# Kept PSUM banks, moved modulation vectors, phase tables by columns on VectorE: a two-layer DiT block on one Trainium2 core

## The chip, the core and the metric

The kernel runs on one core of a Trainium2 chip. A core has TensorE (PE, matmuls into eight PSUM banks of 128 partitions x 512 fp32), VectorE (DVE), ScalarE (ACT), GpSimd (POOL) and SyncE (SP), and 16 DMA engines fed from the queues of SP, ACT and POOL. Each engine works through its own instructions in order and waits on semaphores for the others. The metric is the device time of one execution in microseconds; lower is better.

## What is computed

A network of two layers on 1024 latent tokens and 256 context tokens, width 1024, all in fp32:

```python
for l in range(2):
    mod_l = (silu(c) @ ada_w[l] + ada_b[l]).reshape(b, 6, 1, 1024)      # shift, scale, gate, twice
    h_l = modulate(rmsnorm(x, norm1_g[l]), mod_l[:, 0], mod_l[:, 1])
    o = mla_retention_mixer(...) if l == 0 else s5_mixer(...)
    x = x + mod_l[:, 2] * o
    h_l = modulate(rmsnorm(x, norm2_g[l]), mod_l[:, 3], mod_l[:, 4])
    x = x + mod_l[:, 5] * (square(relu(h_l @ mlp_w1[l])) @ mlp_w2[l])
```

Layer 0 does the same for the context tokens with `mod_c`. The mixer of layer 1 is an S5 state space scan, in both directions, followed by a gated product:

```python
xs = associative_scan(a_bar * x + b_bar u)          # complex, 64 groups of 64 states, per direction
y = einsum('btgp,ghp->btgh', xs, c_mat).real
za, zb = split(gelu(y + d_skip * u) @ w_glu, 2)
out = za * sigmoid(zb)
```

## The kernel before, in words

Every large product is made of three matmuls on split operands (`mm3`): a number is the sum of a high part, rounded by ScalarE, and a low part, the difference, made by VectorE or GpSimd (`hi` and `lo`, line 84). Splitting a weight tile `mraw` gives `uh`, `ul` (first MLP weight, and the weight of the gated product) or `dh`, `dl` (second MLP weight).

The stages follow each other: layer 0's mixer (to about 1090 us), layer 0's MLP (to 2118), the S5 scan (2146 to 2335), the gated product (to 2522), layer 1's MLP (to the end).

`mlp` runs over 16 groups G of two hidden blocks. `first(G)` multiplies the normalised input by two blocks of the first weight, then ReLU and square on ScalarE (`r`, line 1042, and `ah`) and the low part `al` on GpSimd. `second(G-1)` multiplies by the second weight, two blocks deep, into one bank for each of eight output blocks, and VectorE adds each bank, times the modulation, to `x` (line 1064). Layer 0 calls it twice: first for 512 latent and 256 context tokens, then for the other 512 latent tokens. Each bank of `bank()` is one of six in turn (tag `b`); two more (`z`) serve the scan.

Beside layer 0's MLP runs a generator, `side`: the modulation of layer 1 (`ada_rest`: loads `aw` of the transposed weight, multiplied and summed along the row by VectorE, line 215), then the S5 tables: `s5_base` (many small VectorE instructions), `s5_outputs` (GpSimd products `oc`, joined by VectorE at 1383 and 1384, stored to `cst`) with `s5_lags` (small matmuls, stored to `tst`), `s5_inputs` (loads `wb` and `ww`, GpSimd products `wo`, joined by VectorE at 1341 and 1347, stored to `bst`) and `s5_tables` (phases `ta`, `tq`, their sines on ScalarE, stored to `csd`), then two norms. `beat` calls it at a rate of steps per matmul (`RA` in the first call, `RB` in the second), and `later(n, f)` puts a piece off by n steps. From the program so written, the framework makes the order of each engine's instructions at build time; it is that order, not the text, that the engines follow.

`s5_main` takes 32 pairs of groups, two directions each. `states`: TensorE makes `vb` from `ut` and `B`, VectorE turns it by the phase table `CS` (1486), adds two halves (1487), runs two scans (1491), GpSimd multiplies by the table again (`sy`, 1493) and adds two halves (`sa`, 1498; every fourth on VectorE). `outs`: TensorE multiplies `sa` by `C` and `ut` by `T` into banks `z` and `b`, two pairs behind. The `sy` tiles go round three. `glu` transposes the result, splits it (`yh`, `yl`), and makes 16 products of eight `mm3` for each half of the tokens; ScalarE and VectorE gate them and GpSimd adds them to `x`.

Of the kernel before, what the change touches and what calls it, by code (L numbers as in the profile page):

```python
# [9 lines left out]
F32 = mybir.dt.float32  # L10
# [41 lines left out]
class Net:  # L52


    def __init__(self, tc, I, out, tap=None):
        self.tc, self.nc, self.I, self.out = tc, tc.nc, I, out
        self.tap = tap or (lambda *a, **k: None)
        self.top = ExitStack()
        self.gelu = AF.Gelu_apprx_tanh

# [4 lines left out]
    def bank(self, tag="b"):  # L65
        return self.psum.tile([P, 512], F32, tag=tag, name=tag, bufs={"b": 6, "z": 2}[tag])
# [125 lines left out]
    def ada_row(self, tile):  # L192

        r = []
        for s in range(2):
            for k in range(2):
                t = tile(f"silr{s}{k}")
                self.nc.gpsimd.dma_start(
                    t, self.I["crow"][s, 512 * k:512 * k + 512].unsqueeze(0).to_broadcast([P, 512]))
# [4 lines left out]
    def ada_rest(self, tile, rows, todo):  # L204
        nc, I = self.nc, self.I
        for l, j in todo:
            ns = 2 if (l == 0 or j < 2) else 1
            for kt in range(KT):
                for k in range(2):
                    w = tile()  # L210
                    nc.sync.dma_start(w, I["adat"][l, j, kt, :, 512 * k:512 * k + 512])
                    for s in range(ns):
                        m = self.M[:, l, j, kt, s:s + 1]
                        o = w if s == ns - 1 else tile()
                        nc.vector.tensor_tensor_reduce(o, w, rows[2 * s + k], 1.0,
                                                       m if k else self.bias[:, l, j, kt:kt + 1],
                                                       ALU.mult, ALU.add, m)
                    if ns == 2 or k:
# [5 lines left out]
    def rows(self, parts, n):  # L224
# [12 lines left out]
        r = self.bank()  # L237
# [775 lines left out]
    def mlp(self, l, p, chunks, hget, x, beat=lambda w: None, done=None, last=iter(()), after=None, pre=iter(())):  # L1013

        nc, I = self.nc, self.I

# [34 lines left out]

        def second(G, A, w2):
            for t0, n, s in chunks:
                for oc in range(KT):
                    b = self.bank()
                    for fi in range(2):
                        self.mm3(b[:, :n], w2[fi](oc), A[fi, t0], fi == 0, fi == 1)
                    xs = x(oc, t0, n)
                    as_x = (lambda a: a[:, :n]) if len(xs.shape) == 2 else (lambda a: a.rearrange("p (t c) -> p t c", c=P))
                    o = xs  # L1060
                    if G == 15 and done:
                        res = p.tile([P, 512], F32, tag="r", name="res", bufs=2)
                        o = as_x(res)
                    nc.vector.scalar_tensor_tensor(o, as_x(b), self.M[:, l, 5, oc, s:s + 1], xs,  # L1064
                                                   op0=ALU.mult, op1=ALU.add)
                    if G == 15 and done:
# [761 lines left out]
```

## Time and profile before

| | us |
|---|---|
| median of 3 runs (3220.97 to 3245.53) | 3233.07 |
| profiled execution | 3247.53 |
| its span | 3245.7 |
| TensorE busy | 2982.2 (92%) |
| VectorE busy | 2172.1 (67%) |
| ScalarE busy | 1216.8 (37%) |
| GpSimd busy | 1059.6 (33%) |
| mean granted TensorE clock | 0.95 |

A page of the profile first gives the busy time of each engine, then the span in 40 slices of 81 us with a digit for the busy share in tenths. The granted clock is the part of full speed that the throttle let TensorE have. A row of a group reads: line, engine, operation, output <- inputs, shape, count, then busy time and mean nanoseconds of one, then the idle time of the engine just ahead of them and what ended it. A row of a wait reads: who <- whom, microseconds in total, times, longest. A row of a timeline reads: start, duration, engine, line, what, and in brackets the idle time ahead.

### The profile page before, as it was taken

To read this page: it belongs to the slowest core of one execution; us is meant where nothing else is said; L and a number is where in the kernel's file an instruction comes from. 1 tells how busy PE (TensorE), PEld (TensorE's weight loads), DVE (VectorE), ACT (ScalarE), POOL (GpSimd) and SP (SyncE) were. 2 spreads that over 40 slices of the span, in tenths; PEclk is the share of its full clock that TensorE was granted. 3 is DMA by queue.
4 is the path that set the end of the run, shared out by engine and by line. 5 is a ranking of instruction groups with operands and counts; after the bars stand their busy time and mean duration, and the time that the engine had idled before them with its cause. 6 is when DMAs were issued, how large, how long until landed. Compare 5 with 4: busy or idle time off the path is not lost. (4 is left out here: it accounts for less than half of the span.)

```text
span 3245.7 us, 43332 instructions
## 1 busy us (share of the span) xinstructions
PE 2982.2 (92%) x15659; PEld 2447.9 (75%) x15659; DVE 2172.1 (67%) x3899; ACT 1216.8 (37%) x2487; POOL 1059.6 (33%) x1012
## 2 busy tenths in 40 slices
PE   5899998899999999899987799956799999999998
PEld 3777777778878788788876577845588788888887
DVE  6777776687764599756666886479834555555555
ACT  6542322566662322222233455331244422222221
POOL 3642222355450111336526740146522111111111
PEclk8999997899999999999988899977799999999999
DMA  7132222210011356224437556278522111111111
GB/s 248 71 115 83 79 75 62 74 35 25 13 58 60 124 180 212 82 87 122 136 102 210 174 166 144 82 170 201 158 91 91 52 52 52 46 52 46 46 46 65
DMA packets 251927, 323.63 MB, mean 100 GB/s; under 512 B 71504, under 2 KB 166512, under 8 KB 251712
## 3 DMA queue, kind: packets, MB, share of 16 engines
q1 hardware_dynamic: 236432, 293.49, 30.5%
q10 hardware_dynamic: 14272, 24.38, 2.4%
q0 software_dynamic: 1008, 2.99, 0.3%
q8 instruction: 123, 2.02, 0.3%
q14 instruction: 92, 0.75, 0.1%
HBM read 267.43 MB, written 53.35 MB: 99 GB/s over the span
## 5 line engine op out<-in xcount | busy, mean ns | idle before, releaser
L1064 DVE SCALAR_TENSOR_TENSOR x<-b,mods,x 128x512 f32<-128x512 f32 (+1 forms) x624 | 531.4, 876 | 123.0 <-PE b L72 116.9
L84 POOL TENSOR_TENSOR al<-r,ah 128x512 fp32r<-128x512 f32 (+1 forms) x160 | 215.8, 1361 | 1110.4 <-ACT r L1046 1049.0
L70 PE MATMUL b<-ah,dh 128*128 128x512 f32 (+1 forms) x1280 | 481.1, 376 | 24.2 <-DVE x L1064 14.9
L71 PE MATMUL b<-al,dh 128*128 128x512 f32 (+1 forms) x1280 | 476.5, 372 | 0.7 <-POOL al L84 0.7
L72 PE MATMUL b<-ah,dl 128*128 128x512 f32 (+1 forms) x1280 | 474.6, 371 | 0.0
L84 DVE TENSOR_TENSOR ul<-mraw,uh 128x512 fp32r<-128x512 f32 x256 | 204.8, 805 | 388.8 <-ACT uh L76 388.2
L76 ACT ACTIVATE uh<-mraw 128x512 fp32r<-128x512 f32 x256 | 160.8, 629 | 447.2 <-PE b L71 272.7
L72 PE MATMUL b<-h2h,ul 128*128 128x512 f32 (+1 forms) x768 | 283.9, 370 | 35.9 <-DVE ul L84 35.9
L70 PEld LDWEIGHTS b<-ah,dh 128*128 128x128 f32 x1280 | 245.3, 192 | 74.7 <-DVE x L1064 22.1
L70 PE MATMUL b<-h2h,uh 128*128 128x512 f32 (+1 forms) x768 | 284.2, 370 | 14.1 <-ACT uh L76 9.2
L71 PE MATMUL b<-h2l,uh 128*128 128x512 f32 (+1 forms) x768 | 281.0, 366 | 0.0
L71 PEld LDWEIGHTS b<-al,dh 128*128 128x128 f32 x1280 | 245.2, 192 | 41.9 <-POOL al L84 1.1
L72 PEld LDWEIGHTS b<-ah,dl 128*128 128x128 f32 x1280 | 244.3, 191 | 41.5
L84 POOL TENSOR_TENSOR pl<-pe,ph 128x512 fp32r<-128x512 f32 (+1 forms) x128 | 158.8, 1250 | 155.5 <-ACT ph L76 83.8
L76 ACT ACTIVATE dh<-mraw 128x512 fp32r<-128x512 f32 x192 | 117.3, 627 | 238.1 <-PE b L71 222.9
L70 PE MATMUL b<-h3h,uh 128*128 128x512 f32 x512 | 202.2, 396 | 0.0
L71 PE MATMUL b<-h3l,uh 128*128 128x512 f32 x512 | 200.4, 392 | 2.0 <-DVE h3l L312 1.7
L72 PE MATMUL b<-h3h,ul 128*128 128x512 f32 x512 | 201.4, 394 | 0.0
L72 PEld LDWEIGHTS b<-h2h,ul 128*128 128x128 f32 x768 | 149.2, 194 | 65.6 <-DVE ul L84 41.3
L1042 ACT ACTIVATE r<-b 128x512 f32<-128x512 f32 (+1 forms) x160 | 88.0, 550 | 258.8 <-PE b L72 184.8
L70 PEld LDWEIGHTS b<-h2h,uh 128*128 128x128 f32 x768 | 149.0, 194 | 42.7 <-ACT uh L76 11.4
L70 PE MATMUL z<-wh,hh 128*128 128x512 f32 (+1 forms) x400 | 163.1, 408 | 12.6 <-ACT scr L496 6.3
(419 smaller groups left out, 6922.0 us busy)
## 6 DMA issues: line engine op xcount, KB each, us to landing
mraw<-in_w SPq DMA_DIRECT2D x192, 512.0 KB
aw<-in_adat SPq DMA_DIRECT2D x160, 256.0 KB
mraw<-in_glu SPq DMA_DIRECT2D x32, 512.0 KB
CS<-csd SPq DMA_DIRECT2D x32, 320.0 KB
w<-in_adaw SPq DMA_DIRECT2D x32, 256.0 KB
wraw<-in_winr SPq DMA_DIRECT2D x32, 256.0 KB
cst<-oc SPq DMA_DIRECT2D x64, 128.0 KB
wb<-in_s5bt ACTq DMA_DIRECT2D x32, 256.0 KB
```

The source lines that it names most:

```text
L70: mm(o, s[0], m[0], start=start, stop=False)
L71: mm(o, s[0], m[1], start=False, stop=False)
L72: mm(o, s[1], m[0], start=False, stop=stop)
L76: self.nc.scalar.activation(o, x, AF.Copy)
L84: e.tensor_tensor(o, x, h.bitcast(F32), ALU.subtract)
L1042: nc.scalar.activation(r[:, :n], b[:, :n], AF.Relu)
L1064: nc.vector.scalar_tensor_tensor(o, as_x(b), self.M[:, l, 5, oc, s:s + 1], xs, op0=ALU.mult, op1=ALU.add)
```

## The change

- *Banks.* The eight banks become `b` x 4, `c` x 2, `z`, `y`. Outside the layer 0 MLP a ring of six (`bbbbcc`) is handed out as before. Inside, three banks (`c`, `c`, `z`) hold running sums over all 16 groups: six of the eight context blocks in the first call, two to a bank, and three of eight latent blocks in the second. These are added to `x` once, at the end. Everything else rotates over the four `b`.
- *Modulation.* Vectors 3, 4 and 5 of layer 1 leave the side work and are made during the gated product, in loads and sums of 256 columns instead of 512.
- *Tables.* VectorE computes the phases group by group, with the frequency as a scalar; GpSimd has no part in it any more.
- *Queues and delays.* Loads of `s5_inputs` are issued by SP one part ahead (from ACT, in step, before); the stores of `bst`, `cst`, `tst` and `csd` are issued by ACT (SP before). Joins come two steps later (one before), stores five or four (three or two).
- *Scan.* The two halves of `sy` are no longer added; TensorE takes both, with twice as many matmuls. Every third product `sy` is VectorE's. `sy` goes round six tiles, `st` two.

```diff
+        self.ring, self.turn = "bbbbcc", 0
     def bank(self, tag="b"):
-        return self.psum.tile([P, 512], F32, tag=tag, name=tag, bufs={"b": 6, "z": 2}[tag])
+        if tag == "b":
+            self.turn = (self.turn + 1) % len(self.ring)
+            tag = self.ring[self.turn]
+        return self.psum.tile([P, 512], F32, tag=tag, name=tag, bufs={"b": 4, "c": 2, "z": 1, "y": 1}[tag])
...
+        keep, room = {}, 0
+        if kept:
+            self.ring = "bbbb"
+            for t0, n, s in chunks:
+                for oc in range(KT):
+                    if (t0, oc) in kept:
+                        if not room:
+                            bank, room = self.bank("ccz"[len(keep) * n // 512]), 512
+                        keep[t0, oc] = bank[:, 512 - room:512 - room + n], room == 512, room == n
+                        room -= n
...
         def second(G, A, w2):
+            open_ = []
             for t0, n, s in chunks:
                 for oc in range(KT):
-                    b = self.bank()
+                    b, opens, closes = keep.get((t0, oc)) or (self.bank()[:, :n], True, True)
+                    held, end = (t0, oc) in keep, G == 15
                     for fi in range(2):
-                        self.mm3(b[:, :n], w2[fi](oc), A[fi, t0], fi == 0, fi == 1)
...
+                        self.mm3(b, w2[fi](oc), A[fi, t0], fi == 0 and opens and not (held and G),
+                                 fi == 1 and closes and (end or not held))
+                    if end or not held:
+                        open_.append((oc, t0, n, s, b, end))
+                        if closes:
+                            while open_:
+                                add(*open_.pop(0))
...
-            gp.tensor_tensor(t3(a), ib, fb(0), ALU.mult)
-            gp.tensor_tensor(t3(l), ib, fb(1), ALU.mult)
+            for k in range(n):
+                v.tensor_scalar(q[:, cols[k]], self.io, fr[0][k], MAGIC, ALU.mult, ALU.add)
+            v.tensor_scalar(t2(q), t2(q), MAGIC, None, ALU.subtract)
+            for k in range(n):
+                v.scalar_tensor_tensor(a[:, cols[k]], self.io, fr[0][k], q[:, cols[k]], op0=ALU.mult, op1=ALU.subtract)
             yield
-            v.tensor_scalar(t2(q), t2(a), MAGIC, MAGIC, ALU.add, ALU.subtract)
-            v.tensor_tensor(t2(a), t2(a), t2(q), ALU.subtract)
-            v.tensor_tensor(t2(a), t2(a), t2(l), ALU.add)
+            for k in range(n):
+                v.scalar_tensor_tensor(a[:, cols[k]], self.io, fr[1][k], a[:, cols[k]], op0=ALU.mult, op1=ALU.add)
...
-                    nc.sync.dma_start(self.csd[:, g0:g0 + n, 1], t3(q))
+                    nc.scalar.dma_start(self.csd[:, g0:g0 + n, 1], t3(q))
...
+        nx = fetch(*parts[0])
+        for _ in range(4):
+            yield
+        for k, (d, g0) in enumerate(parts):
+            b, w = nx
+            if k + 1 < len(parts):
+                nx = fetch(*parts[k + 1])
+            qs = slice(g0 // 2, g0 // 2 + 4)
+            for r in range(2):
+                x, t = (self.atile(name="wo") for _ in range(2))
+                nc.gpsimd.tensor_tensor(x, w[0], b[r], ALU.mult)
                 yield
...
+                nc.gpsimd.tensor_tensor(t, w[1], b[1 - r], ALU.mult)
+                self.later(2, lambda r=r, x=x, t=t: nc.vector.tensor_tensor(
+                    x, x, t, ALU.add if r else ALU.subtract))
+                self.later(5, lambda qs=qs, d=d, r=r, x=x: nc.scalar.dma_start(self.bst[:, qs, d, r], gpv(x)))
...
-                self.later(1, join)
+                self.later(2, join)
...
+                e = gp if (2 * q + d) % 3 else v
+                e.tensor_tensor(y if d == 0 else y[:, :, :, ::-1],
+                                z[:, :, 31:159].unsqueeze(2).to_broadcast([P, 2, 2, P]), cs[:, :, ::-1, 31:159],
+                                ALU.mult)
+                A[q, d] = y
...
-                for w in range(2):
+                for r, w in ((0, 0), (1, 0), (0, 1), (1, 1)):
...
+                        if kt % 4 == 3:
+                            next(side, None)
...
-            yield from self.ada_rest(lambda: self.atile(name="aw"), rows, [(1, j) for j in range(6)])
+            yield from self.ada_rest(lambda: self.atile(name="aw"), rows, [(1, j) for j in range(3)])
...
+                     kept=[(1024, oc) for oc in range(6)])
...
+                     kept=[(512, oc) for oc in range(3)])
...
+                yield from self.ada_rest(a256, self.ada_row(a256, 1, 256), [(1, 4), (1, 3), (1, 5)], 256)
```

`fetch` issues the four loads of a part, two `wb` and two `ww`, on SP. `add` is the addition to `x` as it stood in `second` before.

What this makes of the engines' orders, at three places. VectorE in the second call of layer 0's MLP, at the phase tables; before:

```order
L1303 TENSOR_SCALAR tq<-ta 128x480
L1304 TENSOR_TENSOR ta<-ta,tq 128x480
L1303 TENSOR_SCALAR tq<-ta 128x480
L84 TENSOR_TENSOR ul<-mraw,uh 128x512
L1305 TENSOR_TENSOR ta<-ta,tl 128x480
L1304 TENSOR_TENSOR ta<-ta,tq 128x480
L1306 TENSOR_SCALAR ta<-ta 128x480
L1305 TENSOR_TENSOR ta<-ta,tl 128x480
L84 TENSOR_TENSOR ul<-mraw,uh 128x512
L1306 TENSOR_SCALAR ta<-ta 128x480
```

And now (`fr` holds the frequencies, `io` the column numbers):

```order
L1328 TENSOR_SCALAR tq<-tq 128x480
L1330 SCALAR_TENSOR_TENSOR ta<-io,fr_12297,tq 128x160 x3
L1333 SCALAR_TENSOR_TENSOR ta<-io,fr_12298,ta 128x160 x3
L1327 TENSOR_SCALAR tq<-io,fr_12297 128x160
L1334 TENSOR_SCALAR ta<-ta 128x480
L1327 TENSOR_SCALAR tq<-io,fr_12297 128x160 x2
L88 TENSOR_TENSOR ul<-mraw,uh 128x512
L1328 TENSOR_SCALAR tq<-tq 128x480
L1330 SCALAR_TENSOR_TENSOR ta<-io,fr_12297,tq 128x160 x3
L1333 SCALAR_TENSOR_TENSOR ta<-io,fr_12298,ta 128x160 x2
L88 TENSOR_TENSOR ul<-mraw,uh 128x512
```

The four instructions of a table group have become eleven, some rows standing for two or three; the splits `ul` and the adds lie between them as before.

VectorE at the end of the scan and the start of the gated product; before:

```order
L1487 TENSOR_TENSOR st<-st 128x320 x2
L1491 SCALAR_TENSOR_TENSOR sz<-R_13200,st 128x160 x4
L1486 TENSOR_TENSOR st<-b,CS 128x640 x2
L1487 TENSOR_TENSOR st<-st 128x320 x2
L1491 SCALAR_TENSOR_TENSOR sz<-R_13200,st 128x160 x4
L1498 TENSOR_TENSOR sa<-sy 128x2x128
L84 TENSOR_TENSOR yl<-b,yh 128x512
L84 TENSOR_TENSOR ul<-mraw,uh 128x512
L84 TENSOR_TENSOR yl<-b,yh 128x512
L84 TENSOR_TENSOR ul<-mraw,uh 128x512
L84 TENSOR_TENSOR yl<-b,yh 128x512 x6
```

And now (an `aw` row is one sum of 256 columns, a `mods` row reads its result out):

```order
L1518 TENSOR_TENSOR st<-st 128x320 x2
L1522 SCALAR_TENSOR_TENSOR sz<-R_12294,st 128x160 x4
L220 ISA aw,mods<-aw,silr_22764,adab 128x256
L220 ISA mods 128x1
L1525 TENSOR_TENSOR sy<-sz,CS 128x4x128
L220 ISA aw,mods<-aw,silr_22767,mods 128x256
L220 ISA mods 128x1
L220 ISA aw,mods<-aw,silr_22764,adab 128x256
L220 ISA mods 128x1
L220 ISA aw,mods<-aw,silr_22770,mods 128x256
```

29 such sums now stand between the last scan and the first `yl`, with the last `sy`, now VectorE's, behind the first of them.

SP at the same place, the loads; before:

```order
L1454 DMA B<-bst 128x512
L1456 DMA CS<-csd 128x2x320
L1457 DMA C<-cst 128x512
L1460 DMA T<-tst 128x1x128 x2
L1003 DMA mraw<-in_glu 128x1024 x32
```

And now:

```order
L1487 DMA CS<-csd 128x2x320
L1488 DMA C<-cst 128x512
L1491 DMA T<-tst 128x1x128 x2
L216 DMA aw<-in_adat 128x256 x29
L1008 DMA mraw<-in_glu 128x1024 x3
L216 DMA aw<-in_adat 128x256 x3
L1008 DMA mraw<-in_glu 128x1024
L216 DMA aw<-in_adat 128x256 x6
```

29 loads for the sums stand ahead of the first weights of the gated product, and more of them between the weights that follow. Elsewhere, of the 32 joins of `s5_inputs` in VectorE's order, 13 now stand in groups 11 and 12 of the first call and 19 at the border between the two calls.

More of the change, by code (lines that the diff above doesn't have):

```diff
@@ L188, in ada_first, with ada_row @@
         self.gains(0, 0)
-    def ada_row(self, tile):
+    def ada_row(self, tile, ns=2, n=512):
         r = []
-        for s in range(2):
-            for k in range(2):
+        for s in range(ns):
+            for k in range(1024 // n):
                 t = tile(f"silr{s}{k}")
                 self.nc.gpsimd.dma_start(
-                    t, self.I["crow"][s, 512 * k:512 * k + 512].unsqueeze(0).to_broadcast([P, 512]))
+                    t, self.I["crow"][s, n * k:n * k + n].unsqueeze(0).to_broadcast([P, n]))
                 self.nc.scalar.activation(t, t, AF.Silu)
@@ L208, in ada_rest @@
             for kt in range(KT):
-                for k in range(2):
+                for k in range(nk):
                     w = tile()
-                    nc.sync.dma_start(w, I["adat"][l, j, kt, :, 512 * k:512 * k + 512])
+                    nc.sync.dma_start(w, I["adat"][l, j, kt, :, n * k:n * k + n])
                     for s in range(ns):
@@ L236, in rows @@
         yield
-        r = self.bank()
+        r = self.bank("b" if len(self.ring) > 4 else "y")
         for j in range(n // P):
@@ new lines, in s5_inputs, with fetch @@
+        parts = [(d, g0) for d in range(2) for g0 in range(0, 64, 8)]
+        def fetch(d, g0):
+            b, w = ([self.atile(name=nm) for _ in range(2)] for nm in ("wb", "ww"))
+            for r in range(2):
+                nc.sync.dma_start(b[r], bass.AP(
+                    tensor=I["s5bt"].tensor, offset=I["s5bt"].offset + (d * 2 + r) * 4096 + g0 * 64,
+                    ap=[[0, 8], [16384, 16], [1, 512]]))
+                nc.sync.dma_start(w[r], bass.AP(
+                    tensor=self.pbd.tensor, offset=self.pbd.offset + (d * 16 + r) * 4096 + g0 * 64,
+                    ap=[[8192, 8], [0, 16], [1, 512]]))
+            return b, w
@@ L1414, in s5_lags @@
         v.tensor_tensor(E[:, 112:P], E[:, 112:P], b[:, P:144], ALU.add)
-        self.later(2, lambda: nc.sync.dma_start(self.tst[4 * it:4 * it + 4].rearrange("g h k -> (g h) k"), E))
+        self.later(4, lambda: nc.scalar.dma_start(self.tst[4 * it:4 * it + 4].rearrange("g h k -> (g h) k"), E))
     def s5_gen(self, gp):
@@ L1514, in outs @@
                         H = slice(64 * h, 64 * h + 64)
-                        mm(o[k][H], A[q, d][R, w, H], C[R, d, w], start=False, stop=d == 1 and w == 1)
+                        mm(o[k][H], A[q, d][R, r, w, H], C[R, d, w], start=False, stop=d == 1 and r == 1 and w == 1)
             if q % 4 == 3:
@@ L1540, in s5_main, with glu @@
         outs(31)
-    def glu(self, p, x, after):
+    def glu(self, p, x, after, side):
         nc, I = self.nc, self.I
@@ L1700, in run @@
             mp = self.pool(st, "mlp0", side="right")
-            self.mlp(0, mp, [(0, 512, 0), (1024, 256, 1)], hget2, x0, beat, last=nrm1(1))
+            self.mlp(0, mp, [(0, 512, 0), (1024, 256, 1)], hget2, x0, beat, last=nrm1(1),
+                     kept=[(1024, oc) for oc in range(6)])
             beat = self.beat(side, RB)
-            self.mlp(0, mp, [(512, 512, 0)], hget2, x0, beat, after=st1.add)
+            self.mlp(0, mp, [(512, 512, 0)], hget2, x0, beat, after=st1.add,
+                     kept=[(512, oc) for oc in range(3)])
         self.drain(side)
@@ L1732, in after, with mods @@
                     next(g0[0], None)
-            self.glu(mp, x, after)
+            a256 = lambda name="aw": self.atile(256, F32, name)
+            def mods():
+                yield from self.ada_rest(a256, self.ada_row(a256, 1, 256), [(1, 4), (1, 3), (1, 5)], 256)
+            mods = mods()
+            self.glu(mp, x, after, mods)
+            self.drain(mods)
             if stop == "glu":
```

83 lines of the change are left out of this document (27 added, 56 removed).

## The prediction

> **What bounds the kernel now.** I read the page first (span, the slices), then the busy times by stretch, then who waits for whom, then the groups. TensorE is busy for 92% of the span, so the question is where the rest is lost. The slices of VectorE and of the granted clock show two holes, slices 20 to 23 and 26 to 28.
>
> ```profile
> span 3245.7 us, 43332 instructions
> DVE  6777776687764599756666886479834555555555
> PEclk8999997899999999999988899977799999999999
> ```
>
> The busy time by stretch (columns: length, then PE, weight loads, DVE, ACT, POOL, granted clock, DMA share, GB/s) puts borders to them: the end of layer 0's MLP, where the side work runs (to 1930), the S5 scan (2146 to 2335), and the gated product behind it.
>
> ```profile
> 1580.00:1710.00 130.00, 116.37 (x667) 99.46 (x666) 80.53 (x119) 36.14 (x69) 47.55 (x35) 0.92 0.41 123
> 1710.00:1820.00 110.00, 84.41 (x324) 65.54 (x323) 75.91 (x78) 33.18 (x58) 76.01 (x52) 0.88 0.68 202
> 1820.00:1930.00 110.00, 96.03 (x374) 73.77 (x373) 99.77 (x151) 66.07 (x122) 64.96 (x48) 0.92 0.58 172
> 2146.00:2335.00 189.00, 127.69 (x1667) 100.97 (x1664) 183.57 (x272) 34.27 (x92) 126.70 (x112) 0.75 0.79 192
> 2335.00:2430.00 95.00, 95.00 (x443) 79.13 (x441) 38.76 (x53) 40.11 (x62) 24.39 (x14) 0.99 0.32 100
> ```
>
> In the scan VectorE is busy 183.6 of 189 us: it sets the pace. From 1820 to 1930 it is busy 99.8 of 110. From 1710 to 1820 nobody is full. TensorE's waits in the MLP (1085 to 2110) name VectorE, though it is not full there; and VectorE's own idle time names GpSimd, and GpSimd's a DMA:
>
> ```profile
> PE b L72 <- DVE ul L84: 35.9, 12, 7.3
> PE b L70 <- DVE x L1064: 19.6, 22, 2.4
> L1383 DVE TENSOR_TENSOR oc<-oc 128x288 f32<-128x288 f32 x32 | 27.1, 846 | 32.8 <-POOL oc L1378 32.7
> L1384 DVE SCALAR_TENSOR_TENSOR oc<-oc 128x288 f32<-128x288 f32 x32 | 21.0, 656 | 20.9 <-POOL oc L1380 20.9
> L1341 DVE TENSOR_TENSOR wo<-wo 128x512 f32<-128x512 f32 x16 | 26.3, 1643 | 35.3 <-POOL wo L1340 35.3
> L1340 POOL TENSOR_TENSOR wo<-ww,wb 128x512 f32<-128x512 f32 x16 | 21.9, 1366 | 31.2 <-DMA ww<-pbd 31.2
> ```
>
> So VectorE stands at a join, in order, with weight splits and adds queued behind it that TensorE needs. How much that costs, the pace tells. The first ReLU of a group starts at these times:
>
> ```profile
> 1151.14 0.60 ACT L1042 ACTIVATE r<-b 128x512 f32<-128x512 f32 x1 [3.74 <-PE b L72]
> 1184.75 0.60 ACT L1042 ACTIVATE r<-b 128x512 f32<-128x512 f32 x1 [3.75 <-PE b L72]
> 1645.96 0.60 ACT L1042 ACTIVATE r<-b 128x512 f32<-128x512 f32 x1 [3.75 <-PE b L72]
> 1728.83 0.60 ACT L1042 ACTIVATE r<-b 128x512 f32<-128x512 f32 x1 [2.54 <-PE b L72]
> 1830.23 0.58 ACT L1042 ACTIVATE r<-b 128x512 f32<-128x512 f32 x1
> 1934.57 0.58 ACT L1042 ACTIVATE r<-b 128x512 f32<-128x512 f32 x1
> 2051.69 0.58 ACT L1042 ACTIVATE r<-b 128x512 f32<-128x512 f32 x1
> 2073.83 0.58 ACT L1042 ACTIVATE r<-b 128x512 f32<-128x512 f32 x1
> ```
>
> Undisturbed, a group of the first call takes 33.6 us (1151.14 to 1184.75) and one of the second 22.1 (2051.69 to 2073.83). Against that pace: group 2 to 15 of the first call takes 494.8 us instead of 13 x 33.6 = 436.8, 58 lost. From 1645.96 to group 1 of the second call there are 82.9 us, with about 62 of work (a third of the first group's 33.6, its two second products of 16.8 each, and one and a half first products of 11): 21 lost. Three groups to 1830.23 take 101.4 instead of 66.4, 35 lost (the inputs); four to 1934.57 take 104.3 instead of 88.5, 16 lost (the tables). Together 130 us.
>
> **The change, part by part.**
>
> *Kept banks.* 6 of 16 adds of a group go in the first call, all 256 wide, and 3 of 8 in the second, 512 wide.
>
> ```profile
> L1064 DVE SCALAR_TENSOR_TENSOR x<-b,mods,x 128x512 f32<-128x512 f32 x104 | 75.4, 743 | 7.4 <-PE b L72 7.3
> L1064 DVE SCALAR_TENSOR_TENSOR x<-b,mods,x 128x256 f32<-128x256 f32 x103 | 45.2, 475 | 0.9 <-PE b L72 0.9
> ```
>
> That is 6 x 0.475 = 2.9 us of VectorE in 33.6, and 3 x 0.743 = 2.2 in 22.1. It is on the path only where VectorE is late. The price: the other products rotate over four banks, not six. A second product lasts 16.8 us for eight wide and eight narrow banks, so about 1.4 per bank of 512 (11 / 8); two banks less are 2.8 us less cover whenever VectorE is held. No row shows four banks. Ends: 0, and 2.8 in each of 31 groups, 87 us. The 22 waits for an add came with six banks and cost 19.6 us, 0.9 each; I take 12, near the low end, since the holds themselves get fewer (next).
>
> *The side work.* Loads of the inputs are issued a part ahead on SP, joins wait two steps instead of one, stores go five steps later from ACT, and 24 steps of modulation leave, so the rest starts earlier. First call: the 53.7 us in which VectorE stands at the `oc` joins, and the first `wo` joins, are the larger part of what the 58 have behind them; the small-operation chain of `s5_base` and the lag matmuls stay. I take 26 of 58 (ends 5 and 50). Border: 7 of 21. Inputs: the waits for `ww` go, and GpSimd remains, two products per join. I take 23 of 35 (ends 5 and 33): GpSimd has 76 of 110 us there, and in the order the last 19 joins stand close together, so some waiting stays. ACT gets 156 stores and loses 64 loads; a store waits for its join, with ReLU and splits queued behind it. Three steps lie between join and store, so I charge nothing; if a join is late by more than that, this cover is gone.
>
> *Tables.* GpSimd loses 44 products; VectorE does eleven instructions for a group of columns instead of four.
>
> ```profile
> L1303 DVE TENSOR_SCALAR tq<-ta 128x480 f32<-128x480 f32 (+1 forms) x22 | 13.1, 594 | 4.3 <-POOL ta L1300 4.3
> L1304 DVE TENSOR_TENSOR ta<-ta,tq 128x480 f32<-128x480 f32 (+1 forms) x22 | 18.1, 821 | 0.1
> L1305 DVE TENSOR_TENSOR ta<-ta,tl 128x480 f32<-128x480 f32 (+1 forms) x22 | 16.8, 763 | 0.1
> L1306 DVE TENSOR_SCALAR ta<-ta 128x480 f32<-128x480 f32 (+1 forms) x22 | 12.3, 559 | 0.0
> ```
>
> Before: 0.594 + 0.821 + 0.763 + 0.559 = 2.74 us per group. After: two of 480 at 0.56 and nine of 160. No row has 160 columns; a third of 0.559 is 0.19, and the 256-wide add above, with a scalar from memory as here, takes 0.475. Nearer to the narrower end I take 0.28: 2 x 0.56 + 9 x 0.28 = 3.6 (ends 2.8 and 5.4). That is 0.9 x 22 = 20 us more VectorE work. Against it, 3 adds less per MLP group, splits no longer slowed by GpSimd, and the order now has four table groups per MLP group where six and a half stood: 4 x 3.6 + 5 x 0.74 + 8 splits of about 0.68 = 23.5 against 22.1. I take 4 us gained of the 16 (ends +25 and -16).
>
> MLP: -26 - 7 - 23 - 4 + 12 = -48.
>
> *S5 scan.* VectorE and GpSimd disturb each other here. Least, middle and longest duration:
>
> ```profile
> L1486 DVE TENSOR_TENSOR st<-b,CS x64: 791/806/825, 2146.5 to 2324.3; 128x640 f32<-128x640 f32 x64
> L1487 DVE TENSOR_TENSOR st<-st x64: 458/477/1008, 2147.4 to 2325.4; 128x320 f32<-128x320 f32 x64
> L1491 DVE TENSOR_TENSOR_SCAN sz<-R,st x128: 456/476/1554, 2148.5 to 2328.0; 128x160 f32<-128x160 f32 x128
> L1493 POOL TENSOR_TENSOR sy<-sz,CS 128x512 f32<-128x512 f32 x64 | 84.2, 1315 | 80.2 <-issue 52.4 <-DVE sz L1491 23.7 <-ACT CS L1469 1.8
> L1498 POOL TENSOR_TENSOR sa<-sy 128x256 f32<-128x256 f32 x48 | 43.8, 924 | 0.2
> ```
>
> Undisturbed, a direction of a pair costs VectorE about 0.73 + 0.40 + 2 x 0.39 = 1.91 us (the least durations less the 0.06 that neighbours overlap), and a quarter of an add, 0.1. It takes 184 / 64 = 2.88. The 0.87 between are what 84.2 + 43.8 = 128 us of GpSimd, 2.0 per direction, do to it: 0.44 of GpSimd's time. After: GpSimd multiplies in two of three, 0.88; VectorE in one of three, 0.6 / 3 = 0.2. So 1.91 + 0.2 + 0.44 x 0.88 = 2.5, and 64 x 2.5 = 160: -24 us. Ends: 0.2 + 1.91 without any disturbance, 135 us, and no gain. TensorE gets 512 small matmuls more (1024 instructions in the trace's count). The existing 1024 are what stands in its 127.7 busy us beside the rest; it waits in this stage, and the clock of 0.75 has room. DMA is busy 0.79 x 189 = 149 us, so below 149 nothing goes unless loads move: 26 of the T loads now stand ahead of the scan. -24 stays above that.
>
> The Trainium skill, SBUF — State Buffer, "Who interferes with whom", has it that a VectorE instruction with two SBUF inputs and a GpSimd one that reads SBUF exclude each other for the whole instruction. By that the disturbance would be all of GpSimd's time; the trace does not agree, for 1.91 + 0.1 + 2.0 = 4.0 would make 257 us of a stage that took 189. Rival B below is what it would do.
>
> *Gated product.* 96 products of 256 come in, 29 of them in the order between the last scan and the first `yl`, and 29 loads stand on SP ahead of the first weights.
>
> ```profile
> 1198.29 0.74 DVE L215 CUSTOM_DVE_ANT_0 aw<-aw,silr,adab 128x512 f32<-128x512 f32 x1
> 1198.96 0.08 DVE L215 DVE_READ_ACCUMULATOR2_ANT mods<- 128x1 f32 x1
> 2326.33 3.19 DVE L1491 TENSOR_TENSOR_SCAN sz<-R,st 128x160 f32<-128x160 f32 x4
> 2330.96 12.17 SPq L1003 DMA_DIRECT2D mraw<-in_glu  x5
> 2335.44 0.69 DVE L84 TENSOR_TENSOR yl<-b,yh 128x512 fp32r<-128x512 f32 x1 [3.54 <-ACT yh L76]
> ```
>
> One of 512 costs 0.67 from start to start; half of it at least, with its fixed part I take 0.40 (ends 0.34 and 0.67): 29 x 0.40 = 11.6 us. Before, 5.9 us lay idle between last scan and `yl`, so 6 remain on the path, and the weights come about as late. The other 67 lie in some nine products of about 5.4 us each (95 us in the row of the stretch, half idle on VectorE): 7.4 x 0.4 = 3 us beside 2 of VectorE work, but 1 MB of loads on top of 0.5, which takes that stretch from 100 to about 270 GB/s. I add 4: +10 (ends 3 and 25). In the first call the 48 products that leave are in the 26 above.
>
> **Sum.** -48 - 24 + 10 = -62. The profiled execution took 3247.5 us (span 3245.7), 14 above the median of 3233.1; off the median, 3171.
>
> **Rivals.** (A) The side work moves but TensorE doesn't win from it: VectorE at 23.5 to 25 per 22.1 us in the tables, and joins that wait on GpSimd near the border. The MLP then gives 15 instead of 48: 3204. For it: VectorE 99.8 of 110 us; against it: the waits named are DMA waits that the change takes away. (B) GpSimd shuts out VectorE for its whole product: the scan takes (2.11 + 0.88) x 64 = 191, +2 instead of -24: 3197. (C) Slower: four banks. If VectorE is held once in each of the 31 groups for longer than the remaining cover, 87 us instead of 12: 3171 + 75 = 3246. It decides from about 74 us, 2.4 per group, upward. For it: adds already made TensorE wait 22 times with six; against: 0.9 us each.
>
> **How the numbers follow.** My forecast and its neighbours 0.66; A 0.15, B 0.09, C 0.10. Ends summed toward each other: MLP -85, scan -35, product +4 give 3117; MLP -12, scan -12, product +18 give 3227. The range 3118 to 3226 leaves C and a tail out. A measurement of this kernel can tell about 1%, 32 us. Faster by over 1% (under 3201): the forecast nearly whole, half of B and part of A, 0.72; within 1%: 0.20; slower: the far part of C, 0.08.
>
> **What would show it.** Right: scan stretch near 160 us with GpSimd near 56 to 60; no DMA wait under `wo`; group pace of the inputs under 26 us; first product after the scan later by 5 to 8 us. Wrong: TensorE's waits for `x` adds well over 20 us (C), ReLU waiting on a join through a store, a table instruction of 160 over 0.4 us, or a gated product over 195 us.

## The result, and the profile after

The changed kernel takes 3304.8 us (median of 4, 3299.4 to 3306.1) against 3234.0 before: a ratio of 1.023, 95% interval 1.0205 to 1.0256. The forecast was 3171, range 3118 to 3226. The profiled execution after lies at the low end of its runs (span 3297.6) and that before at the high end (3245.7), so the traces differ by 52 us only. The same stages, from the first products of each stage in the traces (us):

| | before | after | difference | forecast |
|---|---|---|---|---|
| layer 0's mixer, to the first MLP product | 1090.1 | 1137.6 | +47.5 | 0 |
| layer 0's MLP, first to last `h2` product | 1010.7 | 995.2 | -15.5 | -48 |
| scan, first state product to first `yh` product | 193.5 | 196.9 | +3.4 | -24, and part of +10 |
| gated product, to the first `h3h` product | 184.2 | 195.0 | +10.8 | the other part of +10 |
| layer 1's MLP, to the end | 722.9 | 729.9 | +7.0 | 0 |

Some 44 us between layer 0's MLP and the scan, about the same in both, are not in the table. One trace of a stage is not exact: layer 0's MLP of the kernel before, the same instructions in the same order, took 1000.4 and 1003.8 us in two later traces (`one_score_bank` and `pair_before`, below), so its gain is 5 to 15.5 us.

The page after, first the span, then two rows of the slices. VectorE still has low slices ahead of the scan (16 to 20, 24 and 25, counted from 0); the clock's hole in the scan (slices 26 to 28, 7 before) has gone.

```profile
span 3297.6 us, 45384 instructions
DVE  6776677767754589555548975368864555555545
PEclk8899999899999999999898999989899999999999
```

The busy time by stretch after, with the columns of the table shown before: the outputs (groups 7 to 13 of the first call), the inputs, the tables, the scan, the gated product.

```profile
1383.26:1643.23 259.97, 233.61 (x1675) 195.37 (x1674) 146.72 (x209) 67.97 (x154) 150.42 (x161) 0.96 0.44 136
1797.27:1878.07 80.80, 67.43 (x281) 54.17 (x280) 70.04 (x145) 38.70 (x67) 30.31 (x21) 0.92 0.57 182
1878.07:1967.98 89.91, 87.67 (x379) 70.47 (x378) 80.68 (x194) 55.83 (x101) 11.57 (x8) 1.00 0.57 174
2175.80:2372.70 196.90, 148.64 (x2720) 121.87 (x2720) 168.13 (x341) 41.42 (x103) 59.62 (x46) 0.89 0.82 203
2373.00:2567.70 194.70, 188.92 (x825) 152.01 (x826) 118.30 (x245) 79.22 (x120) 46.91 (x27) 0.98 0.42 131
```

Inputs (three groups, 101.4 before) and tables (four groups, 104.3 before) are shorter. Groups 7 to 13 took 236.0 before and take 260.0 now. (The 243.5 that the expectations below give for before is groups 9 to 15.) VectorE no longer fills the scan, GpSimd's work there has halved, and yet the scan is as long as it was, at a clock of 0.89 instead of 0.75.

The largest loss lies where no line of the change is. The idle time of weight loads ahead of a bank's first product, before and after, in the mixer (input product `z<-wh,hh` and `z<-wh,hl`, scores `z<-qh,kh`):

```profile
L70 PEld LDWEIGHTS z<-wh,hh 128*128 128x128 f32 x400 | 78.9, 197 | 27.7 <-ACT scr L496 6.6 <-ACT hh L298 4.3 <-ACT wh L76 3.1
L72 PEld LDWEIGHTS z<-wh,hl 128*128 128x128 f32 x400 | 78.2, 195 | 19.5 <-DVE hl L299 5.7
L913 PEld LDWEIGHTS z<-qh,kh 98*128 98x128 f32 x176 | 33.5, 190 | 9.7 <-ACT pe L917 3.9
```

```profile
L74 PEld LDWEIGHTS z<-wh,hh 128*128 128x128 f32 x400 | 82.9, 207 | 44.3 <-ACT zr L573 12.5 <-ACT scr L501 10.3 <-ACT hh L303 4.3
L76 PEld LDWEIGHTS z<-wh,hl 128*128 128x128 f32 x400 | 82.1, 205 | 24.3 <-DVE hl L304 8.6
L918 PEld LDWEIGHTS z<-qh,kh 98*128 98x128 f32 x176 | 33.4, 190 | 30.0 <-ACT pe L922 25.5 <-ACT qh L885 0.4
```

Together 56.9 us idle before and 98.6 after, and most of the new part is ended by ScalarE's reads of the bank (`zr`, `scr`, and `pe`, the exponential of the scores). The code tells why: the input product and the score tiles ask for `bank("z")` too. The tag had two banks; the change leaves it one and gives the other, `y`, to the scan and the norms. The description of `z` as the scan's banks, ahead of the prediction, is incomplete.

### The profile page after: what moved, and what is told of

Its sections match the earlier page's. It is cut to its first block, busy times and chain, and to the rows that moved or that the text cites. A ratio compares the mean times of both kernels' runs of the same rounds, so it can differ in the third digit from the quotient of the medians.

```text
span 3297.6 us, 45384 instructions
## 1 busy us (share of the span) xinstructions
PE 3012.1 (91%) x16683; PEld 2447.4 (74%) x16683; DVE 2118.1 (64%) x4014; ACT 1231.6 (37%) x2493; POOL 930.6 (28%) x902
## 5 line engine op out<-in xcount | busy, mean ns | idle before, releaser
L1075 DVE SCALAR_TENSOR_TENSOR x<-b,mods,x 128x512 f32<-128x512 f32 (+1 forms) x400 | 357.9, 918 | 75.5 <-PE b L76 73.7
L74 PE MATMUL b<-ah,dh 128*128 128x512 f32 (+1 forms) x822 | 320.1, 390 | 36.3 <-DVE x L1075 26.4
L75 PE MATMUL b<-al,dh 128*128 128x512 f32 (+1 forms) x822 | 316.3, 385 | 0.7 <-POOL al L88 0.7
L76 PE MATMUL b<-ah,dl 128*128 128x512 f32 (+1 forms) x822 | 315.9, 385 | 0.5 <-DVE dl L88 0.4
L74 PE MATMUL b<-h2h,uh 128*128 128x512 f32 (+1 forms) x768 | 281.6, 367 | 12.1 <-ACT uh L80 11.6
L75 PE MATMUL b<-h2l,uh 128*128 128x512 f32 (+1 forms) x768 | 278.5, 363 | 0.0
L74 PEld LDWEIGHTS b<-ah,dh 128*128 128x128 f32 x822 | 156.1, 190 | 77.4 <-DVE x L1075 36.0
L88 DVE TENSOR_TENSOR dl<-mraw,dh 128x512 fp32r<-128x512 f32 x192 | 150.9, 797 | 50.7 <-ACT dh L80 31.0
L75 PEld LDWEIGHTS b<-al,dh 128*128 128x128 f32 x822 | 156.3, 190 | 29.6 <-POOL al L88 1.1
L76 PE MATMUL z<-wh,hl 128*128 128x512 f32 (+1 forms) x400 | 165.0, 413 | 5.6 <-DVE hl L304 5.6
L75 PE MATMUL z<-wl,hh 128*128 128x512 f32 (+1 forms) x400 | 166.5, 416 | 2.3 <-DVE wl L88 2.3
L75 PEld LDWEIGHTS b<-h2l,uh 128*128 128x128 f32 x768 | 147.8, 192 | 24.2
```

Source lines behind the costliest of these rows:

```text
L74: mm(o, s[0], m[0], start=start, stop=False)
L75: mm(o, s[0], m[1], start=False, stop=False)
L76: mm(o, s[1], m[0], start=False, stop=stop)
L88: e.tensor_tensor(o, x, h.bitcast(F32), ALU.subtract)
```

## The experiments

All ratios are to the kernel before, run beside each set (medians of 3231 to 3234 us).

**1. Two banks for the mixer again.** `two_score_banks` is the changed kernel with

```diff
+        if tag == "z":
+            self.pair = not self.pair
+            tag = "zy"[self.pair]
```

> The changed kernel, with the two PSUM banks z and y taken in turns by the input product and by the attention scores, as the two banks of z were before; in the MLP and the scan nothing differs. Theory (the mixer lost 47.5 us because each product and each score tile now waits until the one bank is read): first MLP matmul back from 1137.6 to 1090 +- 4 us, time 3304.8 - 47 = 3258 (3250 to 3265), scores from 407 back to 379 us. Rival (the mixer lost because the other six banks are now two tags of four and two, taken in turns): first MLP matmul stays at 1130 to 1140 and the time at 3300 to 3306.

`one_score_bank` is the kernel before with `bufs={"b": 6, "z": 1, "y": 1}` and `"zy"[q // 4 % 2]` in the scan alone.

> The kernel before, with one bank for the input product and the scores instead of two; the other is left to the scan, which takes both in turns as before. Theory (one bank costs 47 us by itself): first MLP matmul from 1090 to 1137 +- 5 us, the rest of the kernel unchanged, time 3234 + 47 = 3281 (3272 to 3290). Rival (another part of the change is behind it): 1090 and 3234 within 0.3%.

`two_score_banks`: 3245.4 us (3241.3 to 3254.2), 59 less than the changed kernel, ratio 1.0049 (1.0029 to 1.0069); first MLP product at 1088.9, as forecast. `one_score_bank`: 3304.7, ratio 1.0224 (1.0191 to 1.0256), first MLP product at 1149.4, so the single bank alone makes the kernel before as slow as the whole change does. Its waits for the bank, from the answer on tile `z` in its mixer:

```profile
  ACT zr L568: 17.4, 9
  ACT scr L496: 14.0, 3
  ACT pe L917: 5.8, 11
```

The theory holds; its size was low, and both times missed their forecasts (72 us at the medians for 47 expected, and 59 on the way back). The rivals fall.

**2. Layer 0's MLP.** `stores_on_sp` puts the stores of the side work back on SP; `none_kept` keeps no bank open. Both have the two score banks.

```diff
-                    nc.scalar.dma_start(self.csd[:, g0:g0 + n, 1], t3(q))
+                    nc.sync.dma_start(self.csd[:, g0:g0 + n, 1], t3(q))
...
-            self.mlp(0, mp, [(512, 512, 0)], hget2, x0, beat, after=st1.add,
-                     kept=[(512, oc) for oc in range(3)])
+            self.mlp(0, mp, [(512, 512, 0)], hget2, x0, beat, after=st1.add)
```

> As two_score_banks, with the stores of the side work (cst, tst, bst, csd) issued on SP again instead of ACT; joins and delays stay. Theory (ACT stands at stores whose joins are late, with the ReLU and the weight splits behind it): the six groups of outputs, 260 us from group 7 to 13 in the changed kernel against 243.5 before, fall to 240 to 248, and the time by 12 to 20 us against two_score_banks. Rival (SP is then held by the same joins with the weight loads behind them, as before): outputs within 5 us of 260, or inputs longer by more than 10 us (80.8 to over 90 us for three groups); time within 8 us of two_score_banks or above it.

> As two_score_banks, with no bank kept open in either MLP call: all adds are made in every group, and the other products rotate over six banks again (the norms of the side work keep bank y). Theory (four banks leave TensorE less cover when VectorE is late, my rival C): the six groups of outputs fall from 260 to 248 or less, and the time falls by 10 or more against two_score_banks. Rival (the adds that went are what the tables and inputs gained): outputs within 5 us of 260, tables from 89.9 to 95 to 104 us for four groups, time 10 to 25 us above two_score_banks.

`stores_on_sp`: 3234.5, ratio 1.0007 (0.9987 to 1.0027), 10.9 less than `two_score_banks` where 12 to 20 stood; groups 7 to 13, the outputs, 247.7, inputs 86.7. `none_kept`: 3230.9, ratio 1.0013 (0.9992 to 1.0034). With the next kernel, `one_tag_sp`, which has both edits, they make a square (first to last `h2` product, us):

| | stores on ACT | stores on SP |
|---|---|---|
| banks kept, four for the rest | 995.6 | 985.0 |
| none kept, six for the rest | 979.9 | 984.9 |

Either edit takes away 10 to 16 us, the medians of the times say the same (10.9 and 14.5), and both together take away no more. The last cell also has the single tag; `mods_in_side` and `strict_turns` below, both with the single tag and no kept bank, compare the stores alone: 985.5 on SP, 985.0 on ACT. So it is neither the ring of four nor the stores, but the two at once. How they act together is read from the waits and not shown: ReLU and splits stand on ACT behind a store whose join is late, and with four banks TensorE has less else to do. The waits after, in the MLP:

```profile
ACT dh L80 <- DVE oc L1414: 17.3, 2, 11.4
ACT E L1442 <- DVE oc L1415: 10.4, 4, 6.7
ACT dh L80 <- DVE oc L1415: 8.8, 1, 8.8
ACT r L1058 <- DVE oc L1414: 5.2, 2, 2.9
PE b L74 <- ACT r L1058: 7.0, 4, 4.6
PE b L74 <- DVE x L1075: 26.2, 13, 13.2
```

With the stores on SP no split and no ReLU names a join of VectorE any more, and TensorE's waits for `r` and `uh` fall from 19.4 us (`two_score_banks`) to 9.0; with no bank kept, its waits for the adds to `x` fall from 30.5 to 22.5. The longest single wait, 13.2 us, ends at such an add, ahead of which VectorE stood at a split and at two joins `wo`.

The adds that the kept banks save are worth nothing that the MLP shows: with the stores on SP it takes 985.0 with them and 984.9 without (there with the single tag). `none_kept` missed its forecast at the outputs (251.6 us for six groups where 248 or less stood), though its MLP fell by 15.7.

**3. One tag for six banks, and the moved modulation.** `one_tag_sp` joins both edits of 2 and makes `b` one tag of six instead of `bbbbcc`; `mods_in_side` then takes all of `range(6)` back into the side work, with `mods = iter(())` beside the gated product.

```diff
-        self.ring, self.turn, self.pair = "bbbbcc", 0, True
+        self.ring, self.turn, self.pair = "b", 0, True
-... bufs={"b": 4, "c": 2, "z": 1, "y": 1}[tag])
+... bufs={"b": 6, "z": 1, "y": 1}[tag])
...
-            yield from self.ada_rest(lambda: self.atile(name="aw"), rows, [(1, j) for j in range(3)])
+            yield from self.ada_rest(lambda: self.atile(name="aw"), rows, [(1, j) for j in range(6)])
```

> As none_kept (no bank kept, stores of the side work on ACT, 3230.9 us) with two edits: its stores go back to SP, and the six banks are one tag of six again instead of two of four and two. Theory on the stores (what they hold on ACT adds to what four banks cost): layer 0's MLP, 980 us from first to last product there, falls by another 6 to 10. Theory on the tags (two tags taken in turns let a product wait for an add that one pool of six doesn't): layer 1's MLP, 728 us, goes back to 721 to 724, a group of it from 44.1 to 43.8 us. Together 3214 to 3222. Rivals: the stores only helped where four banks left no cover, then the MLP stays within 3 us of 980; the tags are not the cause of 7 us in layer 1, then it stays at 727 to 730, and the moved modulation is left to blame.

> As one_tag_sp, with all six modulation vectors of layer 1 back in layer 0's side work and none beside the gated product. Theory (the moved vectors cost what they take from the gated product and the end of the scan): first scan product to first gated product 196 to 188 or less, since the 29 sums of 0.41 us and 29 loads in between go; gated product 193.5 to 184; layer 0's MLP longer by 5 to 20 us (48 loads and products more ahead of the outputs); net 0 to -12 us. Rival (the MLP pays as much): the MLP longer by 20 us or more, net slower.

`one_tag_sp`: 3218.7, ratio 0.9966 (0.9947 to 0.9985). Layer 1's MLP goes from 728.0 to 719.5, with the modulation still beside the gated product: the two tags were the 7 us there. (It takes 728.0 to 729.9 in the four traces with two tags, 719.5 to 723.0 in the ten with one.) The waits from 2700 to 3100 us of `two_score_banks`, a stretch in which the kernel before has none on TensorE:

```profile
PEld c L79 <- DVE x L1080: 3.5, 6, 0.7
PEld b L79 <- DVE x L1080: 1.5, 4, 0.5
PEld c L79 <- ACT r L1063: 1.5, 3, 0.5
```

With one tag of six the framework gives a product, when it makes the order, whichever bank it takes to be free, and the ring fixes which tag is next; "in turn", ahead of the prediction, is too strict for the kernel before. The theory on the stores falls, as the square says.

`mods_in_side`: 3194.5, ratio 0.9900 (0.9871 to 0.9928), 24 us less, twice the most that was forecast. Last state product to first `yh` goes from 29.1 to 15.0, the gated product from 192.8 to 184.8, and the MLP, which takes the 48 loads and products back, from 984.9 to 985.5: they cost nothing there. The end of the scan after the change, on VectorE:

```profile
2353.83 1.43 DVE L220 CUSTOM_DVE_ANT_0 aw<-aw,silr,adab 128x256 f32<-128x256 f32 x1
...
2368.33 0.48 DVE L220 CUSTOM_DVE_ANT_0 aw<-aw,silr,adab 128x256 f32<-128x256 f32 x1
2368.74 0.69 DVE L88 TENSOR_TENSOR yl<-c,yh 128x512 fp32r<-128x512 f32 x1
```

The 29 sums, with one product `sy` of 0.7 us among them, hold VectorE for 14.9 us (2353.83 to 2368.74) ahead of the first `yl`.

**4. Why the scan is no faster: loads?** Both kernels are `one_tag_sp` but for one edit. `no_table_load` loads the phase tables of the first three pairs only and uses them for all; `tables_on_act` loads them from ACT's queue, behind the state products of the pair ahead. The edit of the second:

```diff
-            nc.sync.dma_start(CS[:, :, 2:4], self.csd[:, 2 * q:2 * q + 2])
+            nc.scalar.dma_start(CS[:, :, 2:4], self.csd[:, 2 * q:2 * q + 2])
...
+        spread(0)
         for q in range(32):
-            spread(q)
             states(q)
+            if q < 31:
+                spread(q + 1)
```

> As one_tag_sp, but the phase tables of the scan are loaded for the first three pairs only and used again for the rest, so 29 loads of 320 KB out of 36 MB in this stage are left out. Theory (the scan now waits for loads, which SP issues late because it stands at the table's three buffers): first to last product of the scan's inputs from about 170 to 155 us or less, VectorE's idle time there under 10 us. Rival (VectorE and GpSimd still set the pace, by what they do to each other): within 4 us of one_tag_sp.

> As one_tag_sp, but the phase tables of the scan are loaded on ACT's queue, behind the copies for the next pair, and the other three loads of a pair stay on SP. All bytes stay. Theory (SP in order: the loads of B, C, T and the inputs stand behind the wait for a table's buffer): the scan's inputs from about 170 to 160 us or less. Rival (the loads themselves, 36 MB, or the three buffers of the table set the pace): within 4 us of one_tag_sp.

First to last state product: 170.7 in `one_tag_sp`, 172.7 in `no_table_load`, with 151 GB/s in the stage instead of 200, and 188.3 in `tables_on_act`. So in this order of TensorE the loads of the tables don't set the pace, and ACT is a worse place to wait for a table's buffer. Both theories fall (3219.3 and 3230.2 us; ratios 0.998, 0.9954 to 1.0005, and 1.0006, 0.9983 to 1.003).

**5. Why the scan is no faster: TensorE's order.** VectorE's gaps in the scan after come in steps of some 22 us, four pairs; three of seven:

```profile
2218.88 0.82 DVE L1517 TENSOR_TENSOR st<-b,CS 128x640 f32<-128x640 f32 x1 [4.13 <-issue]
...
2241.70 1.55 DVE L1517 TENSOR_TENSOR st<-b,CS 128x640 f32<-128x640 f32 x2 [2.92 <-PE b L1509]
...
2331.89 1.56 DVE L1517 TENSOR_TENSOR st<-b,CS 128x640 f32<-128x640 f32 x2 [3.40 <-PE b L1509]
```

The seven add up to 24 us; for most the profile names a state product as what ended them, for others nothing or the table's load. TensorE's order in the scan, with S for the eight state products of a pair and Q for the sums of one (the first 24 of 64 steps):

```
before    SSSQSQSQSQSQSQSQSQSQSQSQ
after     SSSQQQSSQSSQQQSSSQSQQQSS
```

Before, the two alternate. The code asks for the same turns after, but the framework, which makes the order, puts three pairs' sums in a row (why, no run shows); the newest waits for GpSimd's `sy`, and the state products that VectorE needs stand behind it. `strict_turns` makes TensorE's order alternate, on top of `mods_in_side`, and has the stores on ACT again.

```diff
+        def step(f, q):
+            with (self.tc.issue_after(turn[0].ins) if turn[0] is not None else ExitStack()):
+                f(q)
...
-            states(q)
+            step(states, q)
...
-                outs(q - 2)
+                step(outs, q - 2)
```

> As mods_in_side (3194 us), with two edits in two stages. In the scan, TensorE's order is fixed: a pair's state products, then the sums of the pair two before it, in turns; in the changed kernel's order three to four pairs' sums stand in a row every four pairs, the newest of them waiting for GpSimd, with the next state products behind. Theory (this order is why VectorE idles about 4 us every four pairs): first to last state product from 168.5 to 140 to 152 us, VectorE's gaps under 1 us. Rival (another wait, of the table copies behind the GELU on ACT or of loads, takes its place): 162 us or more. In layer 0's MLP the side work's stores are on ACT again: theory (with six banks for all products the ReLUs that stand behind stores cost nothing): MLP within 6 us of 985; rival (ACT's stores cost in any case): 995 or more. Time if both theories hold: 3172 to 3185 us.

Here `turn[0]` is the last matmul of the step ahead. First to last state product: 152.0 instead of 168.5. The stage to the first `yh` product, first in `mods_in_side`, then in `strict_turns`:

```profile
2103.90:2287.40 183.50, 139.62 (x2720) 115.60 (x2721) 153.30 (x282) 36.73 (x97) 57.78 (x42) 0.95 0.78 193
```

```profile
2120.20:2286.00 165.80, 135.88 (x2720) 116.37 (x2720) 155.92 (x282) 36.70 (x97) 59.41 (x42) 0.91 0.85 213
```

VectorE's work is about the same, its gaps in the scan add up to 4.5 us, one of them 3.15 behind a table copy on ACT, where under 1 us was forecast. The MLP takes 985.0 with the stores on ACT: no cost without kept banks. The time is 3185.3 us, at the upper end of the forecast, ratio 0.9849 (0.9821 to 0.9878), less than that of the kernel before and of the changed one, and 9 less than that of `mods_in_side`, though its mixer, the same instructions as in `mods_in_side`, ended 17 us later in the profiled execution (1092.9).

**6. What is left.** `tables_gpsimd` is `mods_in_side` with the tables made as before the change, `scan_summed` with the scan as before, `pair_before` the kernel before with tag `z` split into two tags in turns (the edit of experiment 1). Of the first edit and then of the second:

```diff
-            for k in range(n):
-                v.tensor_scalar(q[:, cols[k]], self.io, fr[0][k], MAGIC, ALU.mult, ALU.add)
+            gp.tensor_tensor(t3(a), ib, fb(0), ALU.mult)
+            gp.tensor_tensor(t3(l), ib, fb(1), ALU.mult)
...
-                e = gp if (2 * q + d) % 3 else v
-                e.tensor_tensor(y if d == 0 else y[:, :, :, ::-1],
+                gp.tensor_tensor(y.rearrange("p (r w c) -> p r w c", r=2, w=2),
...
+                a = self.atile(256, F32, "sa").rearrange("p (w c) -> p w c", w=2)
+                (v if (2 * q + d) % 4 == 3 else gp).tensor_tensor(a if d == 0 else a[:, :, ::-1], y3[:, 0], y3[:, 1],
```

> As mods_in_side, with the phase tables made as before the change (two products of 480 on GpSimd, four instructions of 480 on VectorE). Theory of the prediction's small gain (tables by columns are worth a few us, as VectorE does more and waits less): layer 0's MLP within 6 us of 985.5, four groups in the table's stretch 91 to 100 us. Rival (they carry most of what the MLP gained, 25 us against before): MLP 1000 us or more.

> As mods_in_side, with the scan as before the change (products all on GpSimd and summed there, three in four, before TensorE). Theory (the scan's edit is worth the 10 us by which first state product to first gated product is shorter than before, 183.5 against 193.5): 190 to 196 us there, time 3201 to 3207. Rival (the shorter stretch has another cause, in what ends the MLP or in the banks): within 3 us of 183.5.

> The kernel before with one edit: the two banks of tag z become two tags of one, taken in turns, in mixer and scan. The instruction order of the mixer is the same. Theory (a forced turn is what brought the first MLP matmul from 1090.1 to 1075.6 in one_tag_sp): 1076 +- 4 there, time 3233 - 14 = 3219 (3212 to 3226). Rival (the 14.5 us came from something else in the change, such as the parting of the norms' bank): 1090 and 3233 within 0.3%.

`tables_gpsimd`: 3211.7, ratio 0.9929 (0.9903 to 0.9955), 17 us more than `mods_in_side`. Its MLP, 988.5, is only 3 us longer, but two things cancel in it. Up to the point where VectorE's orders part, just ahead of the tables, the two kernels run the same instructions in the same order; that took 696.7 us here and 708.1 in `mods_in_side`, a difference between executions. From there to the last `h2` product it took 291.8 us against 277.4 (and 278.5 in `scan_summed`, which has the order of `mods_in_side`). So the tables by columns are worth some 14 us, four groups of them taking 91.1 instead of 101.8; that the whole MLP stayed within the 6 us of the theory is luck.

`scan_summed`: stage of the scan 193.6, 10 us more, as forecast, but the same time, 3193.3, ratio 0.9878 (0.9851 to 0.9906): in TensorE's bunched order the scan's edit is worth nothing that the time shows, and the forecast of 3201 to 3207 was missed. `pair_before`: 3229.8, ratio 0.9987 (0.9965 to 1.0008): no change, the rival holds for the time; its mixer ended at 1084.4, between the two forecasts. Its mixer has the same instructions as that of `one_tag_sp`, so the 14.5 us by which the latter ended earlier than that before lie within what executions differ by.

## Why the prediction was wrong, point by point

- **The step that failed most** is none of the sum: it took the mixer as untouched. The change halves the number of banks of tag `z`, and I followed the tag to the scan only, not to its two other users. Experiment 1 gives 59 to 72 us for it, about the forecast's whole gain of 62, and by itself a loss like the measured one of 71. The rest of the miss, by the table of stages: 32 us of layer 0's MLP, 28 of scan and gated product together, 7 of layer 1's MLP.
- **First call, -26 of 58.** Measured +17 (group 2 to 15: 511.9 against 494.8; 489.2 and 490.1 in the two other traces of the order before). Two errors. Of the 58 "lost" a part was TensorE's own work, which no change of waits gives back: in these groups of the outputs before, it is busy to the last microsecond, 3.5 to 4.8 above 33.6, with 72 to 128 more matmuls:

```profile
1402.42:1439.48 37.06, 37.06 (x267) 32.13 (x266) 21.46 (x32) 11.08 (x24) 15.74 (x19) 1.00 0.25 76
1523.83:1561.13 37.30, 37.30 (x291) 31.86 (x290) 23.98 (x44) 11.40 (x26) 25.41 (x32) 1.00 0.40 119
1561.13:1599.56 38.43, 38.43 (x323) 32.74 (x322) 25.40 (x41) 11.83 (x29) 19.68 (x20) 1.00 0.45 131
```

  The undisturbed group has 195. And "three steps lie between join and store, so I charge nothing" was wrong where there are only four banks; the prediction named this sign ("ReLU waiting on a join through a store"), and the trace shows it. Part of the +17 is also work that came from later groups (7 more of the 32 joins of the inputs).
- **Border, -7.** Measured +3.9 (86.8 against 82.9). Here the stores alone count, not the banks: 87.8 with them on ACT and six banks, 77.2 with them on SP and four. What the border then gains, the three groups behind it lose again in part (86.7 with the stores on SP, 80.8 without).
- **Inputs, -23.** Measured -20.6, and the number is partly luck: of the 32 joins 16 lay in these three groups before and 8 lie there now, the others having moved to earlier groups, which got longer. In `mods_in_side`, with 18 joins there, the three take 95.4, 6 less than before. The group pace, 26.9, missed the sign of "under 26". The mechanism was right: the wait for the loads under GpSimd's product is all but gone (31.2 us before, in the row of L1340):

```profile
L1376 POOL TENSOR_TENSOR wo<-ww,wb 128x512 f32<-128x512 f32 x32 | 52.3, 1634 | 2.0 <-DMA ww<-pbd 1.2 <-DVE wo L1377 0.6
L1377 DVE TENSOR_TENSOR wo<-wo 128x512 f32<-128x512 f32 x32 | 42.8, 1339 | 21.1 <-POOL wo L1376 21.1
```

- **Tables, -4.** The right sign, and too small: the stretch gave -14.4, though with fewer of the table's instructions in it, and `tables_gpsimd` puts some 14 us down to the tables. That is within the end of -16, though VectorE's instructions took longer than forecast, 0.41 us on average for 0.28, and one kind 0.517, over the 0.4 that was to show it wrong; the nine of a group take 3 x (0.312 + 0.517 + 0.391) = 3.7 us. What gains, the waits or GpSimd's products that go, no run parts:

```profile
L1330 DVE SCALAR_TENSOR_TENSOR ta<-io,fr,tq 128x160 f32<-128x160 f32 x64 | 30.1, 517 | 0.7
L1333 DVE SCALAR_TENSOR_TENSOR ta<-io,fr,ta 128x160 f32<-128x160 f32 x64 | 22.5, 391 | 0.0
L1327 DVE TENSOR_SCALAR tq<-io,fr 128x160 f32<-128x160 f32 x64 | 18.0, 312 | 0.0
```

- **Four banks, +12, and rival C (87).** 16 us with the stores on ACT, none with them on SP: nearer to the 12, and only together with the stores. C's size falls, but its sign came: TensorE's waits for the adds rose from 19.6 us to 30.8. That the cost hangs on the stores was not foreseen.
- **Scan, -24.** The engines' part was right: GpSimd 59.6 us where 56 to 60 stood, and in TensorE's old order 152.0 us from first to last state product, 2.4 per direction for 2.5 forecast, 21 less than the 172.7 before, for 24 forecast (165.8 for the whole stage against 193.5). It failed in "So 1.91 + 0.2 + 0.44 x 0.88", which holds only if TensorE delivers on time; the new order of its instructions was there to be read, and the term did not rest on it. Rival B as priced, 191 us, is excluded by 152, but it was priced wrong. It lets GpSimd shut out all of VectorE's work, the product by the phase table (L1486, 0.73 us) too, and that one, which reads a PSUM bank, keeps its length (791 to 825 ns, though GpSimd was busy during nearly the whole of 40 of the 64). The instructions that stretch are the others: a scan took 465 ns with no GpSimd work beside it and 1023 on average with some. Without the 0.73, B gives 64 x (2.11 + 0.88 - 0.73) = 145 us, and the 257 us that the prediction held against whole exclusion becomes 210, still above 189. So the runs don't decide between B in this form and the forecast's 0.44. (B's +2 also counts from 189, the forecast's -24 from 184.)
- **Gated product, +10.** Experiment 3 gives 24 us, within the upper end of 25: the 29 sums take 14.2 for 11.6, the 5.9 idle us counted as their cover gave almost nothing (14.1 us go ahead of the first `yh` product when they go), and the gated product pays 8 for the 4. What it was to pay for, 48 products less in the MLP, was worth nothing.
- **Layer 1's MLP, 0.** +7, from two tags in fixed turns. "Handed out as before" was read from the ring's length. That the modulation beside the gated product was to blame is excluded by `one_tag_sp`, which still has it.
- **Rival A** (3204) was right that the MLP gains little; -15.5 is what it said. Its reason, VectorE full in the tables, was not: the tables gained.

## What to carry to other kernels

Before a change to a pool of buffers is priced, list every place that takes from each tag, in stages far from the change too: a tag cut from two to one cost some 60 to 70 us there. Compare the order of instructions on each engine before and after in every stage a term rests on; a shorter instruction gains nothing if the order bunches its consumer's inputs behind a wait. Count the work in a stretch before its length is called a gain: part of it may have moved next door. And read lost time against what the engine did in it: where it is busy throughout, a pace above the undisturbed one is work, not waiting.

## What the runs showed that was not expected

- A mixer of the same instructions ended between 1074.1 and 1092.9 us in the seven profiled executions from `one_tag_sp` on, `pair_before` aside. Layer 0's MLP of the same instructions agreed to 0.5 us in three traces (`one_tag_sp`, `no_table_load`, `tables_on_act`: 984.9, 984.7, 984.4), but differed by 4 in two others (985.5 and 981.2, `mods_in_side` and `scan_summed`) and by 10 in the three of the kernel before's order. A difference of 15 us in one trace's mixer, or of 5 to 10 in its MLP, is no finding until the medians of the times agree; nearly all of those 10 us lay ahead of the tables.
- In the scan 29 of the 320 KB loads, a quarter of the bytes, could go, in TensorE's bunched order, without a gain in its length (172.7 against 170.7), though the DMA share of the stage is 0.8 with them.
